# Value products of two heads side by side, bias rows read reversed, and a new order of the first microseconds

## The chip, the cores and the metric

One core of one Trainium2 chip runs the whole program: a two-layer block ("block 1") followed by another two-layer block ("block 2"), once. The metric is the device time of one execution in microseconds (us). Three executions of the kernel before gave 2213.95, 2214.05 and 2215.66 us; the median is 2214.05 us. The profile is of one further execution.

## What is computed

A sequence of 256 positions with 1024 features goes through two layers of block 1 and two of block 2. The change lies in block 1 alone. A layer of it, cut to what matters here:

```python
h = rms_norm(x, norm_mix_g[i])                  # (256, 1024)
proj = h @ w_in[i]                              # 10 thousand columns, cut into
q_r, k_r, v_r, g_r, q_n, kv_n, gate_n, m_a, m_b = split(proj)
o_r = retention(rotary(q_r), rotary(k_r), v_r)  # 4 heads
# 16 heads of "nsa" attention, 64 wide, two groups of keys and values:
#   logits of a query with the keys, plus a bias looked up by distance, softmax, times the values,
#   for three branches (compressed blocks, selected blocks, window), gated and added
x = x + mixer(o_r, nsa, m_a, m_b) @ w_out[i]
x = x + ffn(rms_norm(x, norm_ffn_g[i]))
```

The bias of a head depends only on the distance of query and key: `bias[q, k] = table[bucket(q - k), head]`. For 256 positions it is a row of 384 numbers for each head, of which query `q` reads a stretch of 256 that moves by one from query to query.

## The kernel before

**Weights and TensorE.** Activations are held transposed, as a part `hi` rounded to the short fp32 format (fp32r) and the rest `lo`. A weight piece of 512 KB comes in by DMA from SP's queue (`load`, L372), is split by ScalarE (`whi`, L169) and VectorE (`wlo`, L183), and is then multiplied in three products, hi with hi, hi with lo and lo with hi (`mm`, L216). Five raw pieces and six split ones are held. Each engine works through its own list in order, so an instruction that waits holds up all that stands behind it on that engine.

**The order.** `items` is a list of weight pieces and small steps. `execute` runs it, loads pieces and splits them up to `LOOK` ahead, and after each item `bg.pump` lets background generators (`bg`: one for each attention head and retention head) go on. A generator yields at points where it would have to wait; when it goes on is decided by a running estimate of each engine's clock (`eng`, fed by `use`), so the cost that `mm` notes for a product moves later instructions about.

**The start.** `load_x(0)`, a warm-up of `WARM` = 7 products on zeros, the identity matrix (`const_0`), and then the first norm: `Norm.__init__` has the gain row `norm_mix_g` copied to all 128 partitions by a DMA that reads the row 128 times (`bcast_row`, L589, 512 KB), ScalarE squares x (`half`), GpSimd takes the power (`power`, L239), VectorE multiplies x by scale and gain (`scale`, L194), TensorE transposes (`turn`, L250), and ScalarE and VectorE write `hi` and `lo` of it. `norm().both(0)` and `first_turn` do the first 128 positions; `lead` is the item from which weights are loaded and split, and it stands behind the first turn. Then come `load_x(1)`, the norm of the other 128 positions, and `const_1` with the tables for rotary and retention.

**The bias.** `make_bias` computes the 16 rows of 384 numbers by a product and writes them to DRAM as `rb` (L708). `spread(j)` then, for two heads at a time and eight times in all, reads two rows of `rb` into all 128 partitions (L713, `z<-rb`, 384 KB) and writes them out to DRAM as `bd` (L715, 384 KB), both from GpSimd's queue, so that every head has 128 equal rows of 384. `nsa_head` (L873) reads from `bd` with a row step of 383: the diagonal stretch. From the third pair on one `spread` is let go every `PACE` = 9 us, and head `h` begins only when "bias ready" has passed it.

**A head.** `nsa_head(qd, hh)` is head `hh` (0 to 3) of quad `qd` (0 to 3); two heads are under way at a time. Logits come by products with the keys `KH` and `KL`; VectorE adds the bias and takes the minimum in one operation (`add_max`, L203); ScalarE takes the exponential; the result `Z` is scaled, transposed by TensorE into `PT`, and multiplied with the values. That last step, the value products, is four products for a head: two branches, each with 256 and with 128 columns, with `vnat` as weights, 64 columns wide. Full fp32 products are run as two instructions each, so one head has eight instructions `b<-z,vnat`. Their output is the upper or the lower 64 partitions of the bank `O`, as the head's number is odd or even:

```python
if hh == 0: Q["O"] = bank([128, 2, 256])
e, c = hh % 2, hh // 2
o = slice(64 * e, 64 * e + 64)
for br in range(2):
    mm(O[o, c, :], vnat[:, 0, vs], PT[:, 256*br:256*br + 256], ...)
    mm(O[o, c, 128:], vnat[:, 1, vs], PT[:, 512 + 128*br:640 + 128*br], ...)
```

`Z` and `PT` come from a ring of six tiles (`zt`), `bias` from one of four.

Of the kernel before, what the change touches and what calls it, by code (L numbers as in the profile page):

```python
# [18 lines left out]
D = 1024  # L19
# [11 lines left out]
def _const_arrays():  # L31
# [13 lines left out]
    pack(0, [("ident", np.eye(128))])  # L45
# [6 lines left out]
    for h in range(4):  # L52
# [3 lines left out]
             ("decay", np.stack(dec, 1)), ("vmask", p[:, None] // 16 == np.arange(4)[None, :]), ("valid", p >= 31),  # L56
             ("fold", p[:, None] % 32 == np.arange(32)[None, :])])
# [34 lines left out]
WARM = 7  # L92
# [6 lines left out]
PACE = 9.0  # L99
# [3 lines left out]
def tile_kernel(ctx: ExitStack, tc: tile.TileContext, A: dict, out: bass.AP):  # L103
# [111 lines left out]
    def mm(o, lhsT, rhs, start, stop):  # L215
        nc.tensor.matmul(o, lhsT, rhs, start=start, stop=stop, skip_group_check=True)  # L216
        n = width(rhs)
        if rhs.dtype == F32R:
            ns = n / 2.4 * (1 if n >= 256 else 4)
        else:  # L220
            ns = n / 0.6 * width(lhsT) / 128
        use("P", ns, [o], [lhsT, rhs])
# [168 lines left out]
    def execute():  # L391
# [8 lines left out]
        for i, it in enumerate(items):  # L400
# [4 lines left out]
            while nxt < len(specs) and i >= lead:  # L405
# [7 lines left out]
                if turn is not None and sum(1 for q in specs if turn < q < j) >= PAST_TURN:  # L413
                    break
# [179 lines left out]
    class Norm:  # L594


        def __init__(self, row, dst, then=None):
            self.g = u([128, D])
            bcast_row(self.g, row, D)
# [13 lines left out]
        def scale(self, t):  # L613
# [3 lines left out]
            for c in range(2):  # L617
                cs = slice(512 * c, 512 * c + 512)
                self.xn[t, c] = x[:, t, cs] if self.dst is None else w2([128, 512])
                stt(out=self.xn[t, c], in0=x[:, t, cs], scalar=r, in1=self.g[:, cs], op0=OP.mult, op1=OP.mult)  # L620
# [53 lines left out]
    def load_x(t):  # L674
        for c in range(2):
            nc.sync.dma_start(x[:, t, 512 * c:512 * c + 512], xin[:, t, 512 * c:512 * c + 512])

    def begin():
        consts(cp, 0)


    def block1_constants():
        bp = S["bp"]
        consts(bp, 1)
# [5 lines left out]
    def make_bias():  # L690
# [12 lines left out]
        mm(b, tab, oneh[:, :384], True, True)  # L703
        bs = w2([16, 384])
        copy_v(bs, b)

        rb = dr.tile([16, 384], F32, name="rb")
        nc.sync.dma_start(rb, bs)  # L708
        S["bd"] = dr.tile([16, 128, 384], F32, name="bd")

        def spread(j):
            row = zt([128, 2, 384])
            nc.gpsimd.dma_start(row, bass.AP(tensor=rb.tensor, offset=rb.offset + 384 * j,  # L713
                                             ap=[[0, 128], [384, 2], [1, 384]]))
            nc.gpsimd.dma_start(S["bd"][j:j + 2].rearrange("h p k -> p h k"), row)  # L715

# [7 lines left out]
        spread(0)  # L724
# [5 lines left out]
        spread(2)  # L730
        arrives(rv, 12.0)
# [4 lines left out]
        for j in range(4, 16, 2):  # L736
            spread(j)
            S["bias ready"] = j
            step[0] = eng["P"] + PACE
            yield  # L740
        S["bias ready"] = 16

    def block1_layer(i):
# [122 lines left out]
        def nsa_head(qd, hh):  # L866
            g, h, Q = qd // 2, 4 * qd + hh, QD[qd]
            while len(flags) < 2 or S.get("bias ready", 0) <= h:
# [3 lines left out]
            bd = S["bd"]  # L872
            nc.gpsimd.dma_start(bias, bass.AP(tensor=bd.tensor, offset=bd.offset + 49152 * h + 127,  # L873
                                              ap=[[383, 128], [1, 256]]))
# [65 lines left out]
            if hh == 0:  # L940
                Q["O"] = bank([128, 2, 256])
            O = Q["O"]
            e, c = hh % 2, hh // 2
            o = slice(64 * e, 64 * e + 64)
            for br in range(2):
                vs = slice(128 * br + 64 * g, 128 * br + 64 * g + 64)
                mm(O[o, c, :], vnat[:, 0, vs], PT[:, 256 * br:256 * br + 256], c == 0 and br == 0, False)
                mm(O[o, c, 128:], vnat[:, 1, vs], PT[:, 512 + 128 * br:640 + 128 * br], False, False)
            Q["pv"] += 1
# [118 lines left out]
        proj_N(w, 7424, 256, "hT", 8, ev_values, runs=2, stride=384, tmajor=True, between=second_turn)  # L1068
        do(pos_turn)
# [733 lines left out]
    do(load_x, 0)  # L1803
    do(warm_up, WARM)
    do(begin)
    open_pool("block1")
    new_norm(A["norm_mix_g"][0], "hT")
    do(lambda: norm().both(0))
    first_turn("hT")
    lead = len(items)  # L1810
    do(load_x, 1)
# [37 lines left out]
```

## Time and profile before

| what | value |
|---|---|
| median of three executions | 2214.05 us |
| the profiled execution | 2216.03 us |
| its span, first to last instruction | 2214.3 us |
| TensorE busy | 2167.8 us, 98% |
| VectorE busy | 1486.1 us, 67% |
| ScalarE busy | 1236.4 us, 56% |
| moved by DMA | 383.31 MB |
| chain that ended last | TensorE 83%, VectorE 9%, ScalarE 3%, DMA 2% |

The profile shows one execution. PE is TensorE's products, PEld its weight loads, DVE VectorE, ACT ScalarE, POOL GpSimd, SP the engine that issues most DMAs (SPq its queue). A line number is a line of the kernel, often that of a helper (`mm` is L216, `act` L169, `tt` L183), so tiles tell more than lines. A row such as `b<-z,vnat` says that tile b was written from tiles z and vnat. Products are pipelined, and the ends that the profile gives for them are modelled; how long TensorE was taken up by a group is read from its start to the start of the next group. PEclk is the share of TensorE's full clock that was granted: 1.00 is 2.4 GHz, 0.50 is 1.2 GHz.

### The profile page before, as it was taken

How to read it: one execution, taken by the hardware profiler on the slowest of the kernel's cores; microseconds unless marked ns; L12 is line 12 of the kernel's file. 1: busy time of each engine (PE TensorE's matmuls, PEld its weight loads, DVE VectorE, ACT ScalarE, POOL GpSimd, SP SyncE). 2: the span in 40 equal slices, each digit the busy share in tenths (PEclk: the TensorE clock that was granted, in tenths of full speed). 3: DMA queues.
4: the chain of work that ended last, by engine and by line, in shares of the span. 5: the costliest groups of instructions: out<-in, count | busy, mean ns of one | idle time of the engine just before them, and what ended most of it. 6: DMA issues, size and time to landing. Idle time of an engine off the chain costs nothing.

```text
span 2214.3 us, 37531 instructions
## 1 busy us (share of the span) xinstructions
PE 2167.8 (98%) x14692; PEld 1973.1 (89%) x14692; DVE 1486.1 (67%) x2773; ACT 1236.4 (56%) x2044; POOL 115.0 (5%) x131
## 2 busy tenths in 40 slices
PE   8899999999999999999999999999999999989998
PEld 7688899899988888998998999988997999988997
DVE  5677765755576777666555887876557888776555
ACT  4466655544455566554444777655445777555443
POOL 2100100000000000000000010100000000100000
PEclk9999999999999999999999999999999999999999
DMA  9854455565676544555655545455655545455553
GB/s 299 281 150 132 141 153 156 176 199 187 194 223 178 150 139 141 146 180 179 185 187 169 175 134 172 139 174 179 190 188 171 165 144 173 147 163 180 190 186 109
DMA packets 299950, 383.31 MB, mean 173 GB/s; under 512 B 16635, under 2 KB 238987, under 8 KB 299772
## 3 DMA queue, kind: packets, MB, share of 16 engines
q1 hardware_dynamic: 296572, 370.12, 54.2%
q0 software_dynamic: 3200, 10.79, 1.5%
q8 instruction: 115, 1.88, 0.3%
q14 instruction: 63, 0.52, 0.1%
HBM read 376.60 MB, written 4.26 MB: 172 GB/s over the span
## 4 chain that ended last, share of the span: by engine, by line
PE 83%; DVE 9%; ACT 3%; DMA 2%; issue 2%; POOL 1%; SPq 0%; POOLq 0%; DVEq 0%; ACTq 0%
PE b L216 80%; DVE wlo L183 3%; PE b L250 3%; DMA raw<-w_in 2%; DVE u L183 2%; ACT z L169 1%; DVE w L183 1%; POOL s L239 1%; ACT u L169 1%; ACT whi L169 1%; DVE z L194 1%; DVE w L194 0%; DVE z L183 0%; ACT L169 0%; DMA w<-a_lambda 0%
## 5 line engine op out<-in xcount | busy, mean ns | idle before, releaser
L183 DVE TENSOR_TENSOR wlo<-raw,whi 128x1024 fp32r<-128x1024 f32 (+1 forms) x670 | 814.7, 1220 | 449.1 <-ACT whi L169 446.8
L169 ACT ACTIVATE whi<-raw 128x1024 fp32r<-128x1024 f32 (+1 forms) x670 | 704.2, 1056 | 656.8 <-PE b L216 464.7
L216 PE MATMUL b<-u,whi 128*128 128x256 f32 x5760 | 1052.8, 285 | 0.0
L216 PEld LDWEIGHTS b<-u,whi 128*128 128x128 f32 x5760 | 902.6, 192 | 10.0 <-issue 5.3
L216 PE MATMUL b<-u,wlo 128*128 128x256 f32 x2880 | 815.9, 283 | 0.0
L216 PE MATMUL b<-whi,u 128*128 128x512 f32 (+2 forms) x2752 | 811.6, 372 | 1.8 <-ACT whi L169 1.6
L216 PEld LDWEIGHTS b<-whi,u 128*128 128x128 f32 x2752 | 502.0, 189 | 90.9 <-issue 4.9
L216 PEld LDWEIGHTS b<-u,wlo 128*128 128x128 f32 x2880 | 552.7, 192 | 0.0
L216 PE MATMUL b<-wlo,u 128*128 128x512 f32 (+2 forms) x1376 | 509.5, 370 | 0.5 <-DVE wlo L183 0.5
L216 PEld LDWEIGHTS b<-wlo,u 128*128 128x128 f32 x1376 | 260.6, 189 | 39.6 <-DVE wlo L183 1.2
L169 ACT ACTIVATE u<-b 64x512 fp32r<-64x512 f32 (+3 forms) x234 | 133.0, 579 | 101.1 <-PE b L250 52.8
L239 POOL TENSOR_TENSOR s<-s,mhalf 128x1 f32<-128x1 f32 (+3 forms) x60 | 77.5, 1292 | 1508.2 <-DVE s L194 1047.1
L169 ACT ACTIVATE z<-z,s 128x256 f32<-128x256 f32 (+2 forms) x304 | 124.5, 425 | 51.6 <-DVE s L203 39.3
L183 DVE TENSOR_TENSOR u<-b,u 128x512 fp32r<-128x512 f32 (+2 forms) x150 | 98.3, 665 | 21.0 <-ACT u L169 16.8
L169 ACT ACTIVATE w<-b 128x512 f32<-128x512 f32 (+3 forms) x150 | 81.1, 547 | 43.2 <-PE b L216 42.0
L250 PE MATMUL b<-const,w 128*128 128x128 f32 (+1 forms) x416 | 65.3, 280 | 19.5 <-DVE w L194 9.3
L250 PEld LDWEIGHTS b<-const,w 128*128 128x128 f32 (+1 forms) x416 | 47.8, 141 | 31.5 <-issue 13.5
L216 PE MATMUL b<-u 128*128 128x256 f32 (+1 forms) x288 | 42.6, 293 | 14.8 <-ACT u L169 8.6
L169 ACT ACTIVATE u<-w 128x512 fp32r<-128x512 f32 x80 | 49.6, 619 | 11.5 <-DVE w L183 11.5
L216 PEld LDWEIGHTS b<-u 128*128 128x128 f32 x288 | 38.2, 196 | 18.5 <-ACT u L169 9.4
L183 DVE TENSOR_TENSOR w<-w 128x512 f32<-128x512 f32 (+3 forms) x94 | 51.9, 566 | 4.0 <-ACT w L169 3.7
L216 PE MATMUL b<-z,vnat 128*64 128x128 f32 (+1 forms) x256 | 46.8, 332 | 0.0
(145 smaller groups left out, 1233.2 us busy)
## 6 DMA issues: line engine op xcount, KB each, us to landing
raw<-w_in SPq DMA_DIRECT2D x268, 512.0 KB, 3.9
raw<-w_ffn_in SPq DMA_DIRECT2D x80, 512.0 KB, 3.6
raw<-w_up SPq DMA_DIRECT2D x64, 512.0 KB, 3.7
raw<-w_down SPq DMA_DIRECT2D x64, 512.0 KB, 3.5
raw<-w_ffn_out SPq DMA_DIRECT2D x44, 512.0 KB, 3.7
raw<-w_o_ret SPq DMA_DIRECT2D x32, 512.0 KB, 3.4
raw<-w_out SPq DMA_DIRECT2D x32, 512.0 KB, 3.8
raw<-w_o_nsa SPq DMA_DIRECT2D x16, 512.0 KB, 3.4
```

What stands on the lines that cost most here:

```text
L169: nc.scalar.activation(o, i, func, bias=bias, scale=scale, accum_out=accum_out)
L183: nc.vector.tensor_tensor(out=out, in0=in0, in1=in1, op=op)
L194: nc.vector.scalar_tensor_tensor(out=out, in0=in0, scalar=scalar, in1=in1, op0=op0, op1=op1)
L216: nc.tensor.matmul(o, lhsT, rhs, start=start, stop=stop, skip_group_check=True)
L239: nc.gpsimd.tensor_tensor(o, i, mhalf[:, :n], op=OP.pow)
L250: nc.tensor.transpose(o, i, C("ident")[:i.shape[0], :i.shape[0]])
```

## The change

Six edits, all in block 1 or ahead of it:

- **Paired value products.** An even head leaves its `PT` in `Q["PT"]` and ends; the odd head issues both heads' products, alternating: 256 columns of the even head, 256 of the odd, 128 of the even, 128 of the odd, for each branch. The planner books half the time for each (`share` 0.5).
- **Reversed bias rows.** `make_bias` writes the rows to DRAM back to front (`copy_v(bs, b[:, ::-1])`). A head then reads them directly from `rb` with a row step of 1, and takes the tile back to front (`bias[:, ::-1]`) as an operand of `add_max`. All eight `spread`s, `bd` and `PACE` go; heads wait for one flag.
- **The first gain row.** `norm_mix_g` comes in as one row of 4 KB, and TensorE spreads it to 128 partitions by a product with a row of ones, into two PSUM banks; `scale` reads it from there.
- **x in two queues.** The first half of x is issued from SP's queue and the second, with the gain row ahead of it, from ScalarE's, both at the start.
- **One piece ahead of the first turn.** `lead` moves ahead of `first_turn`; `FIRST` = 1 lets one weight piece be split before it. `WARM` is 3.
- **Constants.** Three small tables move from `const_1` to `const_0`; `const_1` is loaded behind the first projection.

The core of the diff:

```diff
-WARM = 7
+WARM = 3
+FIRST = 1
-PACE = 9.0
@@ execute
-                if turn is not None and sum(1 for q in specs if turn < q < j) >= PAST_TURN:
+                if turn is not None and sum(1 for q in specs if turn < q < j) >= (FIRST if turn == lead else PAST_TURN):
@@ Norm
-        def __init__(self, row, dst, then=None):
-            self.g = u([128, D])
-            bcast_row(self.g, row, D)
+        def __init__(self, row, dst, then=None, g=None):
+            if g is None:
+                rows = u([128, D])
+                bcast_row(rows, row, D)
+                g = [rows[:, :512], rows[:, 512:]]
+            self.g = g
@@ begin
+        for q, t in ((nc.sync, 0), (nc.scalar, 1)):
+            if t:
+                row = u([1, D])
+                q.dma_start(row, A["norm_mix_g"][0:1, :])
+            for c in range(2):
+                q.dma_start(x[:, t, 512 * c:512 * c + 512], xin[:, t, 512 * c:512 * c + 512])
+        ones = cp.tile([1, 128], F32, name="ones")
+        nc.vector.memset(ones, 1.0)
+        consts(cp, 0)
+        warm_up(WARM)
+        g = [bank([128, 512]) for _ in range(2)]
         for c in range(2):
-            nc.sync.dma_start(x[:, t, 512 * c:512 * c + 512], xin[:, t, 512 * c:512 * c + 512])
+            mm(g[c], ones, row[:, 512 * c:512 * c + 512], True, True)
+        S["norm"] = Norm(None, Act(8), g=g)
@@ make_bias
-        copy_v(bs, b)
+        copy_v(bs, b[:, ::-1])
-        def spread(j):
-            row = zt([128, 2, 384])
-            nc.gpsimd.dma_start(row, bass.AP(tensor=rb.tensor, offset=rb.offset + 384 * j,
-                                             ap=[[0, 128], [384, 2], [1, 384]]))
-            nc.gpsimd.dma_start(S["bd"][j:j + 2].rearrange("h p k -> p h k"), row)
...
-        for j in range(4, 16, 2):
-            spread(j)
-            S["bias ready"] = j
-            step[0] = eng["P"] + PACE
-            yield
-        S["bias ready"] = 16
+        S["bias ready"] = True
@@ nsa_head
-            nc.gpsimd.dma_start(bias, bass.AP(tensor=bd.tensor, offset=bd.offset + 49152 * h + 127,
-                                              ap=[[383, 128], [1, 256]]))
+            rb = S["rb"]
+            nc.gpsimd.dma_start(bias, bass.AP(tensor=rb.tensor, offset=rb.offset + 384 * h + 1,
+                                              ap=[[1, 128], [1, 256]]))
+            bias = bias[:, ::-1]
...
-            if hh == 0:
+            Q["pv"] += 1
+            if hh % 2 == 0:
+                Q["PT"] = PT
+                return
+            if hh == 1:
                 Q["O"] = bank([128, 2, 256])
+            O, c = Q["O"], hh // 2
+            pair = [(slice(0, 64), Q.pop("PT")), (slice(64, 128), PT)]
             for br in range(2):
                 vs = slice(128 * br + 64 * g, 128 * br + 64 * g + 64)
-                mm(O[o, c, :], vnat[:, 0, vs], PT[:, 256 * br:256 * br + 256], c == 0 and br == 0, False)
-                mm(O[o, c, 128:], vnat[:, 1, vs], PT[:, 512 + 128 * br:640 + 128 * br], False, False)
+                for o, P in pair:
+                    mm(O[o, c, :], vnat[:, 0, vs], P[:, 256 * br:256 * br + 256], c == 0 and br == 0, False, 0.5)
+                for o, P in pair:
+                    mm(O[o, c, 128:], vnat[:, 1, vs], P[:, 512 + 128 * br:640 + 128 * br], False, False, 0.5)
```

The planner places the value products anew. On TensorE, the first of them in the first layer stood by themselves in the kernel before (`z` is the transposed `PT` of one head, `kh`, `kl` the keys, `whi`, `wlo` a weight piece):

```order
L216 MATMUL b_1386<-kh0_166,u_553 128x256
L216 MATMUL b_1386<-kl0_168,u_553 128x256
L216 MATMUL b_1399<-z_1345,vnat_171 64x256
L216 MATMUL b_1399<-z_1345,vnat_171 64x128
L216 MATMUL b_1399<-z_1345,vnat_171 64x256
L216 MATMUL b_1399<-z_1345,vnat_171 64x128
L216 MATMUL b_1410<-whi_1327,u_92 128x512
```

Now the same place, the first value products on TensorE in the first layer, reads:

```order
L216 MATMUL b_1408<-whi_1371,u_95 128x512
L216 MATMUL b_1464<-z_1360,vnat_171 64x256
L216 MATMUL b_1464<-z_1415,vnat_171 64x256
L216 MATMUL b_1464<-z_1360,vnat_171 64x128
L216 MATMUL b_1464<-z_1415,vnat_171 64x128
L216 MATMUL b_1464<-z_1360,vnat_171 64x256
L216 MATMUL b_1464<-z_1415,vnat_171 64x256
L216 MATMUL b_1464<-z_1360,vnat_171 64x128
L216 MATMUL b_1464<-z_1415,vnat_171 64x128
L216 MATMUL b_1401<-whi_1395,u_97 128x512
```

The products of two heads (`z_1360` and `z_1415`) alternate with nothing between them; all 16 pairs of the two layers stand so.

On GpSimd, from the norm of the second 128 positions on, the kernel before has (`rc` holds the compressed branch's bias, `s` small tiles of the norm):

```order
L239 TENSOR_TENSOR s_157<-s_156,mhalf_72 128x1
L723 DMA rc_269<-w_267 128x5x16
L713 DMA z_271<-rb_258 128x768
L728 DMA z_274<-rc_269 128x16x16 x2
L713 DMA z_277<-rb_258 128x768
L715 DMA bd_260<-z_271 128x2x384
L713 DMA z_430<-rb_258 128x768
L715 DMA bd_260<-z_277 128x2x384
```

And now, on the same engine from the same norm on:

```order
L239 TENSOR_TENSOR s_159<-s_158,mhalf_72 128x1
L730 DMA rc_268<-w_266 128x5x16
L734 DMA z_270<-rc_268 128x16x16 x2
L873 DMA bias_1086<-rb_258 128x256
L873 DMA bias_1088<-rb_258 128x256
L873 DMA bias_1438<-rb_258 128x256
```

All transfers `z<-rb` and `bd<-z` (eight of each) are gone, and the heads' reads come directly from `rb`.

On VectorE, the first instructions with data were before:

```order
L194 SCALAR_TENSOR_TENSOR s_104<-s_98 128x1
L194 SCALAR_TENSOR_TENSOR w_108<-x_74,s_105,u_96 128x512
L194 SCALAR_TENSOR_TENSOR w_110<-x_74,s_105,u_96 128x512
L183 TENSOR_TENSOR u_93<-b_112,u_92 128x4x128
L183 TENSOR_TENSOR u_95<-b_119,u_94 128x4x128
L183 TENSOR_TENSOR wlo_130<-raw_126,whi_129 128x1024
L183 TENSOR_TENSOR wlo_137<-raw_133,whi_136 128x1024
```

The first instructions of VectorE with data are now:

```order
L194 SCALAR_TENSOR_TENSOR s_108<-s_99 128x1
L183 TENSOR_TENSOR wlo_120<-raw_116,whi_119 128x1024
L194 SCALAR_TENSOR_TENSOR w_112<-x_74,s_109,b_91 128x512
L194 SCALAR_TENSOR_TENSOR w_114<-x_74,s_109,b_92 128x512
L194 SCALAR_TENSOR_TENSOR s_158<-s_100 128x1
L194 SCALAR_TENSOR_TENSOR w_162<-x_74,s_159,b_91 128x512
L183 TENSOR_TENSOR u_96<-b_126,u_95 128x4x128
L183 TENSOR_TENSOR u_98<-b_133,u_97 128x4x128
L194 SCALAR_TENSOR_TENSOR w_164<-x_74,s_159,b_92 128x512
L183 TENSOR_TENSOR wlo_141<-raw_123,whi_140 128x1024
```

The split of the first weight piece (`wlo_120`) has moved ahead of the norm's products with x, and three instructions of the other positions' norm (`s_158`, `w_162`, `w_164`) ahead of the second piece's split (`wlo_141`).

## Rows read from the trace of the kernel before

**Rows 1.** Page: busy us, share, instructions by engine; ScalarE's weight splits.

```profile
PE 2167.8 (98%) x14692; PEld 1973.1 (89%) x14692; DVE 1486.1 (67%) x2773; ACT 1236.4 (56%) x2044; POOL 115.0 (5%) x131
...
L169 ACT ACTIVATE whi<-raw 128x1024 fp32r<-128x1024 f32 (+1 forms) x670 | 704.2, 1056 | 656.8 <-PE b L216 464.7
```

**Rows 2.** Stretches: length, busy us (count) by engine, PEclk, DMA share, GB/s.

```profile
0.00:5.00 5.00, 3.53 (x8) 2.86 (x9) 0.73 (x4) 2.68 (x5) 0.19 (x4) 1.00 0.45 150
5.00:10.00 5.00, 2.52 (x12) 1.97 (x11) 1.41 (x2) 0.00 (x0) 0.55 (x1) 0.86 0.94 324
...
50.00:70.00 20.00, 19.81 (x149) 16.69 (x147) 11.18 (x15) 8.55 (x12) 7.45 (x12) 1.00 1.04 390
70.00:80.00 10.00, 2.42 (x9) 2.13 (x10) 8.82 (x11) 6.16 (x8) 0.00 (x0) 0.67 1.07 367
80.00:90.00 10.00, 10.00 (x49) 7.89 (x48) 3.44 (x8) 4.46 (x9) 0.00 (x0) 0.81 0.69 210
110.00:290.00 180.00, 180.00 (x1160) 158.64 (x1159) 139.69 (x416) 119.53 (x263) 15.68 (x25) 1.00 0.48 142
```

**Rows 3.** TensorE in time: start us, us, instruction, [idle before <-releaser].

```profile
138.44 1.51 PE L216 MATMUL b<-z,vnat 128*64 128x256 f32 x8
139.88 0.50 PE L216 MATMUL b<-whi,u 128*128 128x512 f32 x1
...
290.65 2.22 PE L216 MATMUL b<-z,vnat 128*64 128x256 f32 x16
292.80 0.39 PE L216 MATMUL b<-u,whi 128*128 128x256 f32 x1
...
370.92 1.51 PE L216 MATMUL b<-z,vnat 128*64 128x256 f32 x8
...
957.50 1.51 PE L216 MATMUL b<-z,vnat 128*64 128x256 f32 x8
```

**Rows 4.** Tile vnat: instructions, duration min/median/max, first and last start.

```profile
L216 PE MATMUL b<-z,vnat x256: 272/326/431, 138.4 to 958.7; 128*64 128x256 f32 x64, 128*64 128x128 f32 x64
```

**Rows 5.** TensorE in time: an attention of block 2 with alternating halves.

```profile
1275.55 0.88 PE L216 MATMUL b<-z,V 128*64 128x256 f32 x8
1276.35 0.39 PE L216 MATMUL b<-u 128*128 128x256 f32 x1
```

**Rows 6.** TensorE in time, 69 to 79 us.

```profile
69.42 0.39 PE L216 MATMUL b<-whi,u 128*128 128x512 f32 x1
77.29 0.79 PE L216 MATMUL b<-u 128*128 128x256 f32 x2 [7.49 <-ACT u L169]
78.37 1.01 PE L216 MATMUL b<-u 128*128 128x256 f32 x3 [0.28 <-DVE u L183]
```

**Rows 7.** Chain that ended last, 30 to 90 us: start, us, what.

```profile
57.74 12.82 DMA raw<-w_in
```

**Rows 8.** DMA of 0 to 100 us: queue; issues, KB, median to landing.

```profile
q0 software_dynamic: 1856, 7.12, 19.5%
...
z<-rb POOLq DMA_DIRECT2D x8, 384.0 KB, 7.9
bd<-z POOLq DMA_DIRECT2D x8, 384.0 KB, 6.8
```

**Rows 9.** TensorE in time, its early waits and the first product of layer 1.

```profile
12.66 0.80 PE L216 MATMUL b<-whi,u 128*128 128x512 f32 x1 [1.63 <-ACT whi L169]
...
40.04 0.67 PE L216 MATMUL b<-z 128*128 128x512 f32 x1 [0.75 <-DMA z<-rc]
...
622.19 0.48 PE L216 MATMUL b<-whi,u 128*128 128x512 f32 x1
```

**Rows 10.** VectorE in time, 8 to 18 us.

```profile
8.25 1.41 DVE L194 SCALAR_TENSOR_TENSOR w<-x,s,u 128x512 f32<-128x512 f32 x2 [3.29 <-DMA u<-norm_mix_g]
...
12.64 4.63 DVE L183 TENSOR_TENSOR wlo<-raw,whi 128x1024 fp32r<-128x1024 f32 x4 [0.25 <-ACT whi L169]
```

**Rows 11.** Tile bias: bias additions, duration min/median/max, first and last start.

```profile
L203 DVE CUSTOM_DVE_ANT_0 z<-b,bias x128: 248/285/294, 121.6 to 948.9; 128x128 f32<-128x128 f32 x128
```

## What the change will do to the time

> **What bounds the kernel now.** I began with the shares on the page: TensorE is busy for 98% of the span, VectorE for 67% [rows 1]. That is an average, so I went on to the table of stretches. From 110 to 290 us, where the first layer's heads run, TensorE is busy for all of 180 us at the full clock, while VectorE is idle for 40 of them and DMA works at half its share [rows 2]. There, time is what TensorE is given to do. The stretch from 70 to 80 us is the exception: TensorE is busy for 2.4 of 10 us, the DMA engines are full (share 1.07, as in the 20 us before), and the granted clock falls to 0.67 and stays low into the next stretch [rows 2]. TensorE's own rows show one wait of 7.49 us [rows 6], and the chain of waits leads from it, through the splits and rotary steps that stand in VectorE's list, back to a weight piece that was issued at 57.74 us and took 12.82 us to land [rows 7]. At the very start a third picture: VectorE waits 3.29 us for the copied gain row, and TensorE's first real product starts at 12.66 us [rows 9, 10]. The sum below has a term for each of the three.
>
> **Paired value products.** Each head has eight instructions, 256 in all, so 32 heads [rows 4]. A head by itself occupies TensorE from 138.44 to 139.88 us, 1.44 us; all lone heads look like this. Two places have two heads back to back in their old order, 2.15 us from 290.65 to 292.80 [rows 3]. So 28 lone heads and two doubles cost 28 x 1.44 + 2 x 2.15 = 44.6 us. What a pair in the new form costs is shown by an attention of block 2 that already writes the upper and the lower half of a bank with the same shapes: its eight instructions, one branch of two heads, take from 1275.55 to 1276.35, 0.80 us [rows 5]. A lone head needs 1.44 us for two branches, so if its first branch costs 0.80 like that pair's, its second costs 0.64; the pair takes no longer than the lone head, and the halves run at the same time. I take 1.45 us for a pair with both branches. Sixteen pairs: 23.2 us. The term is **-21.4 us**. It lies on the path whole, because TensorE has no idle time in these stretches. Ends: 1.35 us a pair by the two doubles, where overlap goes on through the middle of the group (-23), and 1.80 for the rival below (-15.8). What covers the rest: VectorE's work is not less, and its 140 us then stand in about 170 instead of 180 us, still with idle time.
>
> TensorE's list in block 2 has the alternating products in another order (256 and 128 columns of one half, then of the other), and the row of 0.80 us says that the halves overlap even so [rows 5]. The Trainium skill, in "TensorE: Matmul & The Clock Gate", section "Part 3: Packing small matmuls — row/col tiling", says that products start and end strictly in program order and only weight loads are pulled ahead. By that rule two full-fp32 products, each two passes, would overlap only where the second pass of one half meets the first of the other, and the pairs would give 15.8 instead of 21.4 us. The row speaks against it here; it is kept as a rival.
>
> **Spreads and the bias.** Eight reads `z<-rb` and eight writes `bd<-z` of 384 KB go [rows 8]: 16 x 0.393 = 6.3 MB of the 7.12 MB that the software queue moved. At the 390 GB/s of 50 to 70 us [rows 2] that is 16 us of full DMA, all of it ahead of the wait at 69.7 us or beside it. The wait is 7.49 us, so twice as much transfer goes as is needed to end it. With it go 0.28 us of idle at 78.37 [rows 6] and the low clock after it: 0.81 over 80 to 90 us is 3.8 us at half clock [rows 2], and the 2.7 us from 77.29 to 80 are at half clock too; less the idle, 6.2 us of which half are lost, 3.1. Together 7.5 + 0.3 + 3.1 = **-10.9 us**. A further 0.75 us, the wait for `z<-rc` at 40.04 [rows 9], goes with the full queues: **-0.75**. What is late next there is TensorE itself. `const_1` (786 KB, 2 us of DMA) stands later in SP's queue than before, ahead of the pieces for 30 us on; it is not needed before the rotary steps. Bounds: nothing gained but half of the wait (-5.5), and, on the other side, all that the first layer takes longer than the second. From its first product to its last value product the first layer takes 370.92 - 12.66 = 358.3 us, the second 957.50 - 622.19 = 335.3 [rows 3, 9]; the 23 us are the most that this and the next part could give.
>
> Per head the read from `rb` moves as much as that from `bd`. It is issued 3 us of planner's time ahead, and a later landing would hold VectorE, which has slack, before TensorE. Reading an operand back to front is not in the trace. The bias additions take 285 ns [rows 11], 192 in all with a second form; I take no change, since each still reads one element after the other, and price the opposite below.
>
> **The start.** The copied gain row (512 KB) goes and the second half of x takes its place ahead of the first weight piece, so about as many bytes stand before it: two halves of x, 0.084 of constants and the piece, 1.66 MB. By 5 us 0.75 MB had moved, and then 324 GB/s [rows 2], which puts the piece at 5 + 0.91/0.324 = 7.8 us. VectorE's list now has that piece's split ahead of the norm's products: 7.8 + 1.06 (ScalarE) [rows 1] + 1.16 (VectorE, 4.63/4) [rows 10] = 10.0 us, where before the norm's products began at 8.25. From there to the first product it was 12.66 - 8.25 = 4.4 us; the split on ScalarE (1.06) and the second half of the norm (about 0.7, half of 1.41 us) no longer stand in between, which leaves 2.6 and puts the first product at about 12.6 us: no earlier. What remains is that both parts of the first piece are ready and that the second turn's work is done in between, against three norm instructions (1.5 us) that now stand ahead of the second piece's split. I take **-1 us**, with -2.5 (piece at 7.0 us) and +2 (piece where it was, above 9 us, everything behind it) as ends. The two spreading products and the shorter warm-up lie in TensorE's wait and cost nothing; the clock was low after the long warm-up too (0.86 over 5 to 10 us [rows 2]), so I expect the same low start. ScalarE issues three DMAs ahead of its table load, some 1.3 us, while x is on its way.
>
> **Sum.** -21.4 - 10.9 - 0.75 - 1.0 = -34. The profiled execution took 2216.03 us (span 2214.3 and 1.7 around it), 2.0 more than the median of 2214.05; against the profile the sum gives 2182, against the median **2180 us**.
>
> **Rivals.**
> - *Halves only overlap in part.* Products issue in strict order. Count a pass of 256 columns as a step: a lone head takes 6 steps in 1.44 us, two heads one after the other 12, and a pair in which only the second pass of one half meets the first of the other 7.5, which is 1.80 us; 16 x 1.80 = 28.8, and the saving is 44.6 - 28.8 = 15.8: **2186 us**. For it: no trace of before has this very order of full-fp32 pairs. Against it: the 0.80 us of [rows 5].
> - *The DMA wait stays in part, or the start comes late.* Weight pieces, x and `const_1` alone fill the queues, or the first piece lands at 9 us: 5 to 8 us less, **2185 to 2188**. Against it: 6.3 MB less, and the next layer has no such wait.
> - *More goes.* If the first layer becomes like the second save for its bias products, 5 to 10 us more: **2170 to 2175**.
> - *Held tiles.* The even head's `PT` stays in the ring of six until the odd one is done; two heads under way hold four, so five of six are in use. If that delays each pair by 0.5 to 1 us, **2188 to 2196**.
> - *Slower: VectorE becomes the bound.* If an operand read back to front is slow, 96 additions a layer grow. VectorE's idle time of 40 us from 110 to 290 [rows 2], less the 11 by which the stretch shrinks, is used up at +0.31 us each; from +0.49 us (2.7 times as long) the gain is gone, and at three times (+0.57) it is 2 x (55 - 30) = 50 us against the 34: **2230 us**.
>
> **How the numbers follow.** Forecast, 2175 to 2185: 0.62. More goes: 0.12. DMA or start in part: 0.12. Partial overlap: 0.06. Held tiles: 0.03. Slower by VectorE: 0.05. The range 2170 to 2188 leaves out the last two and the edges of the others. About 0.2%, 4.4 us, is what a measurement of this kernel can tell from no change; all cases but the last lie beyond it on the fast side, so faster 0.94, same 0.01 (a half-slow VectorE), slower 0.05.
>
> **What would show it.** In the profile of the changed kernel: 16 groups of sixteen value products at about 1.45 us each; if they take 1.8, it is the partial overlap. No idle of TensorE above 1 us between 20 and 300 us, and a granted clock of 1.00 from 70 to 90 us; a wait there with DMA share near 1 would be the second rival. Less software-queue traffic by 6.3 MB. First product between 11 and 14 us. Bias additions at 285 ns; if they are at 600 or more and VectorE is full from 110 to 290 us, the last rival has come. The prediction would be wrong if TensorE showed waits on `PT` or bias tiles in the heads' stretches.

## The result, and the profile after

| | kernel before | changed kernel |
|---|---|---|
| median of four executions each | 2214.86 us | 2179.26 us |
| lowest to highest | 2213.95 to 2216.77 us | 2178.75 to 2181.48 us |
| ratio of the times, 95% interval | | 0.984, 0.9823 to 0.9857 |
| span of the profiled execution | 2214.3 us | 2177.6 us |
| chain that ended last: TensorE, VectorE, DMA | 83%, 9%, 2% | 86%, 8%, 0% |

The change takes 35.6 us off; 2180 had been forecast. The page of the changed kernel: busy us, share and instructions by engine, then DMA queues with packets, MB and share, then the chain by engine.

```profile
PE 2142.6 (98%) x14688; PEld 1957.2 (90%) x14688; DVE 1487.1 (68%) x2774; ACT 1235.2 (57%) x2044; POOL 100.5 (5%) x115
...
q0 software_dynamic: 1664, 4.50, 1.2%
...
PE 86%; DVE 8%; ACT 3%; issue 1%; POOL 1%; DMA 0%; POOLq 0%; SPq 0%; DVEq 0%; ACTq 0%
```

TensorE is busy for 25.2 us less than in [rows 1]; the rest of the 36.7 us of span is its idle time. The software queue moves 4.50 MB over the whole span, 10.79 before: the 6.3 MB of the spreads are gone.

Stretches of the changed kernel: length, busy us (count) of PE, PEld, DVE, ACT and POOL, PEclk, DMA share, GB/s.

```profile
30.00:50.00 20.00, 20.00 (x165) 18.83 (x164) 14.30 (x31) 11.14 (x18) 4.49 (x6) 1.00 1.08 311
50.00:70.00 20.00, 20.00 (x151) 17.19 (x150) 16.56 (x22) 9.70 (x12) 0.00 (x0) 1.00 0.92 284
70.00:80.00 10.00, 10.00 (x55) 7.48 (x57) 5.47 (x11) 6.03 (x10) 0.00 (x0) 1.00 0.71 223
80.00:90.00 10.00, 10.00 (x57) 7.46 (x50) 5.56 (x9) 3.94 (x6) 0.79 (x2) 1.00 0.57 163
110.00:290.00 180.00, 180.00 (x1226) 162.15 (x1225) 142.41 (x447) 124.73 (x288) 13.25 (x25) 1.00 0.53 149
```

Against [rows 2]: TensorE fills 70 to 80 us, where it had 2.42 of 10; the clock is 1.00 in all of these stretches; the DMA share from 50 us on is 0.92 and falling, where it had been 1.04 and then 1.07.

TensorE of the changed kernel in time, around the first pair of value products: start us, us, instruction.

```profile
132.23 0.39 PE L216 MATMUL b<-whi,u 128*128 128x512 f32 x1
132.55 1.52 PE L216 MATMUL b<-z,vnat 128*64 128x256 f32 x16
134.00 0.50 PE L216 MATMUL b<-whi,u 128*128 128x512 f32 x1
134.34 0.40 PE L216 MATMUL b<-wlo,u 128*128 128x512 f32 x1
134.57 0.62 PE L216 MATMUL b<-whi,u 128*128 128x512 f32 x2
```

Two heads take from 132.55 to 134.00, 1.45 us; one head took 1.44 [rows 3]. All 16 groups look like this, 23.2 us in all.

Tile bias of the changed kernel: the additions (duration in ns min/median/max) and the landing of its transfers.

```profile
L203 DVE CUSTOM_DVE_ANT_0 z<-b,bias x128: 249/286/293, 108.7 to 908.8; 128x128 f32<-128x128 f32 x128
...
DMA to landing us min/median/max: 3.1/3.6/8.3
```

286 ns read back to front, 285 front to back [rows 11].

The start of the changed kernel, on ScalarE, VectorE and TensorE, one answer each: start us, us, instruction, idle before and its releaser.

```profile
8.40 1.06 ACT L169 ACTIVATE whi<-raw 128x1024 fp32r<-128x1024 f32 x1 [2.35 <-DMA raw<-w_in]
```

```profile
9.48 1.23 DVE L183 TENSOR_TENSOR wlo<-raw,whi 128x1024 fp32r<-128x1024 f32 x1 [3.25 <-ACT whi L169]
10.63 1.40 DVE L194 SCALAR_TENSOR_TENSOR w<-x,s,b 128x512 f32<-128x512 f32 x2
```

```profile
11.42 1.97 PE L250 MATMUL b<-const,w 128*128 128x128 f32 x8 [3.18 <-DVE w L194]
13.22 0.79 PE L216 MATMUL b<-whi,u 128*128 128x512 f32 x1
13.81 0.63 PE L216 MATMUL b<-wlo,u 128*128 128x512 f32 x1
```

The piece was there at 8.40 us instead of 7.8, and the first product came at 13.22 instead of 12.6. The 0.59 us between two products of 512 columns, against 0.34 and 0.23 in the stretch above, point to the low clock. The profile's clock column reads 1.00 there, but in e7 below, which has the same instructions up to there and the same 0.59 us, it reads 0.50 from 10 to 15 us.

**A ledger by landmarks.** TensorE's order differs between the kernels, but GpSimd takes the same powers for the norms in both. GpSimd of the kernel before, at three of them (first retention norm, norm ahead of the feed-forward part of layer 1, the last norm):

```profile
95.20 0.57 POOL L239 TENSOR_TENSOR s<-s,mhalf 128x1 f32<-128x1 f32 x1
...
1010.38 0.56 POOL L239 TENSOR_TENSOR s<-s,mhalf 128x1 f32<-128x1 f32 x1 [116.61 <-DVE s L194]
...
2187.71 1.46 POOL L239 TENSOR_TENSOR s<-s,mhalf 128x1 f32<-128x1 f32 x1 [6.12 <-DVE s L194]
```

The same in the changed kernel:

```profile
82.25 0.57 POOL L239 TENSOR_TENSOR s<-s,mhalf 128x1 f32<-128x1 f32 x1
...
973.50 0.56 POOL L239 TENSOR_TENSOR s<-s,mhalf 128x1 f32<-128x1 f32 x1 [116.43 <-DVE s L194]
...
2151.13 1.47 POOL L239 TENSOR_TENSOR s<-s,mhalf 128x1 f32<-128x1 f32 x1 [6.11 <-DVE s L194]
```

The same way for every kernel below, in us ahead of the kernel before (a minus is behind; the second column is the feed-forward norm of layer 0, 423.79 us before):

| kernel | 95 us | layer 0 | layer 1 | end | time, us |
|---|---|---|---|---|---|
| changed kernel | 13.0 | 25.0 | 36.9 | 36.6 | 2179.26 |
| e1, pairs alone | 3.6 | 15.8 | 27.7 | 24.2 | 2193.05 |
| e2, reversed bias alone | 12.2 | 12.4 | 12.4 | 9.8 | 2202.78 |
| e3, start alone | 4.5 | 4.6 | 4.7 | 3.4 | 2211.63 |
| e10, spreads back as traffic | 6.8 | 18.3 | 30.2 | 29.5 | 2190.49 |
| e8, spreads further apart | 5.0 | -11.4 | -11.4 | -11.4 | 2228.28 |
| e5, pairs not alternating | 12.0 | 18.4 | 24.6 | 24.2 | 2192.09 |
| e6, alternating by branch | 12.8 | 24.5 | 35.9 | 35.2 | 2181.01 |
| e7, planner's share 1.0 | 13.5 | 25.4 | 37.3 | 34.7 | 2181.73 |
| e4, no piece ahead of the turn | 11.6 | 23.7 | 35.6 | 34.4 | 2181.80 |
| e9, longer warm-up | 14.0 | 26.0 | 38.0 | 35.1 | 2180.21 |
| changed kernel, second profile | 12.5 | 24.5 | 36.4 | 35.9 | 2180.60 |

So 13.0 us come before 95 us, 12.0 in layer 0, 11.9 in layer 1, and block 2 gives back 0.3. Each row is one execution, set against one execution of the kernel before; how far two executions of the same instructions lie apart is seen in the first experiments.

### The profile page after: what moved, and what is told of

Read it like the earlier page. It is cut to its first block, busy times and chain, and to the rows that moved or that the text cites. A ratio compares the mean times of both kernels' runs of the same rounds, so it can differ in the third digit from the quotient of the medians.

```text
span 2177.6 us, 37496 instructions
## 1 busy us (share of the span) xinstructions
PE 2142.6 (98%) x14688; PEld 1957.2 (90%) x14688; DVE 1487.1 (68%) x2774; ACT 1235.2 (57%) x2044; POOL 100.5 (5%) x115
## 4 chain that ended last, share of the span: by engine, by line
PE 86%; DVE 8%; ACT 3%; issue 1%; POOL 1%; DMA 0%; POOLq 0%; SPq 0%; DVEq 0%; ACTq 0%
PE b L216 83%; PE b L250 3%; DVE wlo L183 3%; DVE u L183 2%; ACT z L169 1%; ACT u L169 1%; POOL s L239 1%; DVE w L183 1%; ACT whi L169 1%; DVE z L194 1%; DVE w L194 0%; DVE z L183 0%; ACT L169 0%; DVE z L1408 0%; DVE s L208 0%
## 5 line engine op out<-in xcount | busy, mean ns | idle before, releaser
L239 POOL TENSOR_TENSOR s<-s,mhalf 128x1 f32<-128x1 f32 (+3 forms) x60 | 73.1, 1219 | 1505.8 <-DVE s L194 1045.5
L183 DVE TENSOR_TENSOR u<-b,u 128x512 fp32r<-128x512 f32 (+2 forms) x150 | 98.2, 665 | 13.6 <-ACT u L169 10.8
L169 ACT ACTIVATE w<-x 128x512 f32<-128x512 f32 x44 | 27.4, 624 | 33.3 <-DVE x L183 30.6
```

The lines of the kernel that those rows point to most:

```text
L169: nc.scalar.activation(o, i, func, bias=bias, scale=scale, accum_out=accum_out)
L183: nc.vector.tensor_tensor(out=out, in0=in0, in1=in1, op=op)
L239: nc.gpsimd.tensor_tensor(o, i, mhalf[:, :n], op=OP.pow)
```

## The experiments

**Each part alone: e1, e2, e3.** e1 is the kernel before with the paired products of the diff and `share`; e2 is it with the reversed rows, without `spread` and `bd`; e3 is it with the edits of the start (gain row, x in two queues, `FIRST`, `WARM`, constants). Their diffs are the matching pieces of the one shown ahead.

> The kernel before with the paired value products alone. Theory (halves of the array run at the same time, TensorE is the limit): 16 groups of sixteen value products at 1.45 us, 21.5 us less there, 21 to 24 us in all, about 2191 to 2193 us, and the 7.5 us wait near 70 us stays. Rival (the pairs only pay off because the DMA wait went, or the held tiles cost something without the other edits): less than 15 us.

> The kernel before with the reversed bias rows alone: no spreads, heads read from rb. Theory (the spreads' 6.3 MB fill the DMA queues): the wait of 7.5 us near 70 us and the half clock behind it go, 10.9 + 0.75 = 11 to 12.5 us less, about 2202 to 2204 us; bias additions stay at 285 ns. Rival (the wait comes from the weights and const_1 alone): under 5 us.

> The kernel before with the edits of the start alone (gain row spread by TensorE, x in two queues, one piece ahead of the first turn, warm-up of 3, const_1 later). Theory: the start itself gives about 1 us (0 to 2.5), 2212 to 2215 us, and the wait near 70 us stays at 6 to 8 us. Rival (the bytes that are moved or spared at the start, half a megabyte, shorten the wait near 70 us): 3 us or more.

Measured: e1 2193.05 us, ratio 0.9902 (0.9885 to 0.9918); e2 2202.78, 0.9947 (0.9932 to 0.9962); e3 2211.63, 0.9983 (0.9973 to 0.9992). TensorE of e1 in time, with the wait near 70 us:

```profile
74.54 0.80 PE L216 MATMUL b<-u 128*128 128x256 f32 x2 [5.28 <-ACT u L169]
```

Stretches of e2:

```profile
50.00:70.00 20.00, 20.00 (x153) 17.23 (x151) 16.89 (x24) 10.83 (x13) 0.00 (x0) 1.00 0.96 307
70.00:80.00 10.00, 10.00 (x54) 7.85 (x53) 6.06 (x10) 5.27 (x10) 0.00 (x0) 1.00 0.68 213
```

TensorE of e3 in time (its line numbers are one higher):

```profile
40.67 1.10 PE L217 MATMUL b<-z 128*128 128x512 f32 x2 [2.98 <-issue]
...
72.17 0.51 PE L217 MATMUL b<-u 128*128 128x256 f32 x2 [1.74 <-ACT u L170]
```

e2 by itself ends the wait and the low clock after it. It is 12.2 us ahead at 95 us, and its median is 12.7 us below the 2215.50 us of the kernel before in the same series. e1 gains 12.2 and 11.9 us in the two layers; its median is 22.4 us lower.

The first column needs care. Up to 95 us, e1 has the same instructions in the same order as the kernel before, on every engine and in every DMA queue: its value products come later. Still it is 3.6 us ahead there, with a wait of 5.28 us where [rows 6] has 7.49. So these 3.6 us are a difference between two executions and not an effect of the pairs. With the spreads in place, the length of the wait near 70 us varies. Without them, five profiles whose lists are the same up to 95 us (the changed kernel's two, e5, e6, e7) stand at 12.0 to 13.5.

What the weight pieces took to land shows where the wait comes from. DMA issues of pieces from 45 to 70 us, in the kernel before, e1, e2 and the changed kernel: size of one, median us from issue to landing.

```profile
raw<-w_in SPq DMA_DIRECT2D x8, 512.0 KB, 13.8
```

```profile
raw<-w_in SPq DMA_DIRECT2D x8, 512.0 KB, 10.9
```

```profile
raw<-w_in SPq DMA_DIRECT2D x11, 512.0 KB, 5.2
```

```profile
raw<-w_in SPq DMA_DIRECT2D x9, 512.0 KB, 4.9
```

With the spreads a piece takes two to nearly three times as long. e3 still has them, and its pieces take 11.1 us. It has two waits, 1.74 us near 70 us and 2.98 at 40.67. The piece that its chain waits for was issued at 51.81 us and took 13.63 us, against 57.74 and 12.82 in [rows 7]: it came earlier, not faster. By its median e3 is 3.9 us lower (1.8 to 6.0 by the interval of its ratio). In the changed kernel the start adds less: 12.0 to 13.5 us at 95 us, against 12.2 for e2, is a gain between -0.2 and 1.3. Whether the start edits also shorten the spreads' wait, one profile of each can't tell from the difference between executions.

**The traffic alone: e10, e8.** e10 is the changed kernel with the sixteen spread transfers put back, which nobody reads; e8 is the kernel before with the spreads further apart.

```diff
+        S["bd"] = dr.tile([16, 128, 384], F32, name="bd")
+        def spread(j):
+            row = zt([128, 2, 384])
...
+        spread(0)
...
+        spread(2)
...
+        for j in range(4, 16, 2):
+            spread(j)
+            step[0] = eng["P"] + 9.0
+            yield
```

And e8:

```diff
-PACE = 9.0
+PACE = 27.0
```

> The changed kernel with the sixteen transfers of the spreads put back, whose result nobody reads; the heads still read rb and wait for one flag. Theory (bytes in the queues made the wait): a TensorE wait of several us near 70 us comes back, with DMA share near 1.05 from 30 to 70 us, 7 to 12 us more than the changed kernel, about 2186 to 2191 us. Rival (the wait came from the gate and the pace of 9 us, or from heads that waited for bd): 0 to 2 us more.

> The kernel before with PACE = 27 instead of 9: the same sixteen spread transfers, but the last six pairs come three times as far apart in the planner's clock. Theory (the wait near 70 us is the bias traffic in front of the weight pieces): the DMA share over 50 to 70 us falls from 1.04 to 0.95 or less, the wait of 7.5 us shrinks below 3 us, and by the GpSimd landmark at 95 us the kernel is 5 to 12 us ahead of the kernel before; time 2203 to 2211. Rival (what counts is the long chain of a spread's landing, rb to tile to bd, not how much stands in the queues): the wait near 70 us stays at 6 us or more, time 2213 to 2218. Third: the heads are held back by the late rows and the planner fills with other work, which moves waits to 100 to 200 us.

Measured: e10 2190.49 us (ratio 0.9885, 0.9871 to 0.99), e8 2228.28 (1.0056, 1.0039 to 1.0072). Stretches of e10:

```profile
50.00:70.00 20.00, 17.41 (x129) 14.30 (x127) 16.30 (x23) 11.70 (x16) 6.17 (x10) 1.00 1.04 396
70.00:80.00 10.00, 9.30 (x41) 7.48 (x42) 3.97 (x7) 4.98 (x8) 0.00 (x0) 0.66 1.10 349
```

TensorE of e10 in time:

```profile
70.42 0.79 PE L216 MATMUL b<-u 128*128 128x256 f32 x2 [3.01 <-ACT u L169]
```

Weight pieces of e10 from 45 to 70 us, as above:

```profile
raw<-w_in SPq DMA_DIRECT2D x9, 512.0 KB, 9.7
```

No engine but GpSimd, which issues them, waits for these transfers, and up to 95 us the lists of all other engines are those of the changed kernel. Still the wait is back, the clock falls, a piece takes 9.7 us to land instead of 4.9, and by 95 us 13.0 - 6.8 = 6.2 us are lost (5.2 to 6.7 against the five profiles above). The profiled execution is the fastest of e10's four, 2186.45 us; by the medians the loss is 11.2 us. It is the transfers in the queues that hold up the weight pieces.

In e8 only five of the eight pairs are out before 56 us, its weight pieces land in 8.0 us, and its wait near 70 us is down. TensorE of e8 in time, at 70 us and later:

```profile
73.23 0.50 PE L216 MATMUL b<-u 128*128 128x256 f32 x2 [2.16 <-ACT u L169]
...
274.00 0.33 PE L250 MATMUL b<-const,z 128*128 128x128 f32 x1 [2.71 <-DVE z L188]
...
378.51 1.36 PE L250 MATMUL b<-const,z 128*128 128x128 f32 x4 [3.52 <-ACT z L169]
```

That gives 5.0 us by 95 us, but only 1.4 more than e1, whose lists are those of the kernel before; and the DMA share over 50 to 70 us is 1.05, where the theory had 0.95 or less. So e8 fits the theory in part and does not decide by itself. Its time missed the forecast. The rows of the later heads come late (the last pair is read at 202.88 us on GpSimd), the last heads' value products run until after 390 us instead of 371, and TensorE waits for the heads' own steps at 274 and 378 us. From 380 to 390 us no weight products are left to lie between them. In all, 16.4 us are lost in layer 0. That is the third outcome, later than forecast.

**The order within a pair: e5, e6, e7.** e5 issues all eight products of the even head and then all eight of the odd one; e6 issues, for each branch, 256 and 128 columns of the even head, then of the odd one; e7 has `share` 1.0. The diffs against the changed kernel, in this order:

```diff
-            for br in range(2):
-                vs = ...
-                for o, P in pair:
+            for o, P in pair:
+                for br in range(2):
+                    vs = ...
                     mm(O[o, c, :], ...)
-                for o, P in pair:
                     mm(O[o, c, 128:], ...)
```

```diff
                 for o, P in pair:
                     mm(O[o, c, :], ...)
-                for o, P in pair:
                     mm(O[o, c, 128:], ...)
```

```diff
-        use("P", ns * share, [o], [lhsT, rhs])
+        use("P", ns, [o], [lhsT, rhs])
```

> The changed kernel with the sixteen value products of a pair in another order: all eight of the even head, then all eight of the odd one, still back to back. Theory (the two halves run at the same time when products of both are near each other in TensorE's list; how far apart they may stand is the question): as in the two doubles of the kernel before, 2.15 us a group instead of 1.45, that is 16 x 0.7 = 11 us more than the changed kernel, about 2190 us. Rival (any order back to back overlaps in full): 1.45 us a group and no change, 2179 us. Rival (strict program order): 2.7 us a group, 20 us more.

> The changed kernel with the order of block 2 within each pair: for a branch 256 and 128 columns of the even head, then 256 and 128 of the odd one. Theory (products of the two halves overlap over a distance of four instructions, as block 2's 0.80 us a branch shows): 1.45 to 1.6 us a group, 0 to 2 us more than the changed kernel, 2179 to 2182 us. Rival (strict program order): 1.8 us or more a group, 6 us or more.

> The changed kernel with the planner booking the whole time for each product of a pair (share 1.0 instead of 0.5), so that the order of the instructions differs but not their number. Theory (what the pairs give is run time on TensorE, not the planner's order): 16 groups of sixteen at 1.45 us, no wait above 1 us from 20 to 300 us, time 2177 to 2185. Rival (the planner's order gave a part): a new wait between 100 and 400 us, the end of layer 0 at least 2 us later than in the changed kernel, time 2186 or more.

Measured, one execution each: 2192.09, 2181.01 and 2181.73 us. TensorE of e5 in time, the first group:

```profile
133.50 2.22 PE L216 MATMUL b<-z,vnat 128*64 128x256 f32 x16
135.66 0.50 PE L216 MATMUL b<-whi,u 128*128 128x512 f32 x1
```

Value products of that group that are at work from 133.45 to 134.20 us, and from 134.38 to 134.42 (duration in ns min/median/max, first and last start):

```profile
L216 PE MATMUL b<-z,vnat x4: 272/326/430, 133.5 to 134.1; 128*64 128x256 f32 x2, 128*64 128x128 f32 x2
...
L216 PE MATMUL b<-z,vnat x2: 379/405/431, 134.2 to 134.2; 128*64 128x256 f32 x2
```

And e6, the same group:

```profile
132.73 1.57 PE L216 MATMUL b<-z,vnat 128*64 128x256 f32 x16
134.24 0.50 PE L216 MATMUL b<-whi,u 128*128 128x512 f32 x1
```

e6 takes 1.50 us a group, close to the 1.45 of full alternation; e5 takes 2.15, which is what two adjacent heads took before. In e5 four products start alone, the first with 430 ns, the next of 256 columns with 379. At 134.2 us two of 256 columns begin together, with 379 and 431. The second is the odd head's first, ninth in TensorE's list: it starts beside the even head's fifth, ahead of three that stand before it. So the even head's second half and the odd head's first half run together, and the overlap reaches over about four products; e6's distance of two is within it. That each engine works through its list in order, as the part on the kernel before has it, does not hold for TensorE's two halves here. The Trainium skill, "TensorE: Matmul & The Clock Gate", section "Part 3: Packing small matmuls — row/col tiling", says that products start and end strictly in program order; by that, e6 could overlap only where its halves meet, and e5 in one place. The rows of both disagree with it for the start. e7, with another order of the rest, has the same 1.45 us groups and no wait; its ledger is 0.4 to 0.5 us ahead of the changed kernel's up to layer 1. What the pairs give is TensorE's own time and not the planner's order.

**The start: e4, e9.** e4 is the changed kernel with `FIRST` = 0; e9 has four more warm-up products behind the spreading ones, in TensorE's wait. e9 was run once, and then four times beside the unaltered changed kernel; the table has it by its second profile.

```diff
-FIRST = 1
+FIRST = 0
```

```diff
+        warm_up(4)
         S["norm"] = Norm(None, Act(8), g=g)
```

> The changed kernel without a weight piece split ahead of the first turn. Theory (the norm's products stand behind that split in VectorE's list and wait for it from about 8.0, when scale and gain are ready, to 10.63 us): they start near 8 us, the first transposes near 9 us instead of 11.42, the first product of weights at 11 to 12.5 us instead of 13.22; 0 to 2 us less. Rival (the edit pays): the first product has to wait for the split afterwards, at 13 us or later, and nothing or less than nothing is gained.

> The changed kernel with four more products on zeros behind the two that spread the gain row, in TensorE's wait from 8.2 to 11.4 us. Theory (TensorE's clock goes to full the sooner the less it idles before): the products of 512 columns follow each other at 0.23 us from about 13 us on instead of from 16.6, 1 to 2.5 us less. Rival (the clock rises no sooner): 0.42 us a product until 16 us or later, and no change or up to 1 us more where the zeros' products hold up the transposes.

> The kernel of e9_warm_more, timed: four more warm-up products behind the spreading ones, in TensorE's wait for the norm. In its single look the spacing of products was that of the full clock from 13.1 us (16.6 in the changed kernel) and the landmark at 95 us stood 1.3 us earlier, while the end stood where the changed kernel's stands. Theory: the 1.3 us are real and the two later half-clock stretches of block 2 vary between executions, so over five rounds 2176 to 2179, 1 to 2 below the changed kernel of the same job. Rival: block 2 gives them back each time, and the two agree within 0.5 us.

> The changed kernel unaltered, on the same chip as e9_timed, as its measure: 2178.5 to 2181.5 as in its first runs. The half-clock stretches of block 2 should stand at other places or have other lengths than in its first profile if they vary between executions, and at the same places if they hang on the order of the work.

Measured: e4 2181.80 us (one execution); e9 2179.83 (one execution) and then 2180.21 (median of four, ratio 0.9836, 0.9822 to 0.9851); the changed kernel beside it 2180.60 (0.9838, 0.9823 to 0.9853). TensorE of e4 in time:

```profile
11.83 0.80 PE L216 MATMUL b<-whi,u 128*128 128x512 f32 x1 [1.63 <-ACT whi L169]
...
20.93 0.50 PE L216 MATMUL b<-wlo,u 128*128 128x512 f32 x1
21.27 0.62 PE L216 MATMUL b<-whi,u 128*128 128x512 f32 x2
```

TensorE of e9, timed:

```profile
8.17 3.78 PE L216 MATMUL b<-w 128*128 128x256 f32 x8
11.74 1.92 PE L250 MATMUL b<-const,w 128*128 128x128 f32 x8
13.49 0.55 PE L216 MATMUL b<-whi,u 128*128 128x512 f32 x1
13.88 0.40 PE L216 MATMUL b<-wlo,u 128*128 128x512 f32 x1
```

e4's first product comes 1.4 us before the changed kernel's, but its products stand at the spacing of half clock until 20.9 us (16.6 in the changed kernel), and at 95 us it is 0.8 to 1.3 us behind the two profiles of the changed kernel, 0.3 to 1.8 behind the five that share their lists up to there. The early split is worth about that, as far as one execution shows. e9 fills TensorE's wait; its products follow at 0.39 us from 13.5 us on and at the full clock's spacing from 13.9, and it is 1.5 us ahead of the second profile at 95 us and 1.6 at the end of layer 1. At the end it is 0.8 behind. Stretch 1170 to 1190 us of e9, and then of the changed kernel beside it (columns as above):

```profile
1170.00:1190.00 20.00, 17.91 (x86) 14.97 (x86) 13.90 (x23) 12.05 (x17) 1.95 (x2) 0.91 0.48 136
```

```profile
1170.00:1190.00 20.00, 17.79 (x90) 14.52 (x90) 13.62 (x22) 12.87 (x21) 1.96 (x2) 1.00 0.41 123
```

Both wait 2.09 us for VectorE here, at 1176.7 and 1178.3. In e9 the granted clock falls behind it, in the other kernel it doesn't. Block 2 took most of e9's lead back in both of its profiles, and the two times agree: the rival in its expectation. No experiment gave a time measurably below the changed kernel's.

## Why the prediction was right, point by point

- **Paired value products: right.** 16 groups of 1.45 us were forecast and measured. The choice between 1.45 and 1.80, which went by the row of another attention [rows 5] against the rule of strict order, was the right one; e5 and e6 show why. The layers give 12.0 and 11.9 us, though, where the groups alone explain 10.8 each (read start to start, they add up to 22.4 us a layer before and 11.6 now). The other 1.1 to 1.2 a layer had no term. In the rows above, a value product starts 0.32 us after the `whi` product before it, and the one behind the group takes 0.34, where weight products among themselves follow at 0.23: each border of a group costs up to 0.1 us, and there are 16 groups where there were 30. e5 agrees: a layer before has 14 lone groups and a double, 22.4 us, and e5 has 8 x 2.15 = 17.2; the 5.2 between them are less than the 6.4 and 6.2 that it gains. That the borders are all of it is argued from these rows, not tried apart.
- **Spreads: right in mechanism, and in size within what varies.** 10.9 + 0.75 = 11.65 us were forecast; e2 has 12.2 at 95 us against the profile of before, 8.6 against e1's, and 12.7 by its median (8.4 to 15.1 by the interval of its ratio). The term was read from one wait of 7.49 us; e1's 5.28 for the same instructions would have made it 2.2 smaller by the wait alone. e10 shows that the transfers do it, without any wait of TensorE for them. "Twice as much transfer goes as is needed" held: without the spreads nothing is late in their place, and TensorE no longer waits there.
- **The start: the size is about right, the working only in part.** -1 was taken; 13.0 - 12.2 = 0.8 came out, 0.3 by the second profile, and these are within the 1.5 us by which profiles with the same lists differ. The piece landed 0.6 us later than worked out, and all behind it moved by the same 0.6. That the first product comes no earlier held. That the second turn's work done in between pays all the same is borne out by e4, in one execution. The expectation for e3 that the wait near 70 us would stay at 6 to 8 us was wrong, and its time came out below the forecast; why is open, as said there.
- **Slack of the heads: right.** From 20 to 420 us TensorE's waits come to 0.4 us in all, none on `PT` or on bias tiles; VectorE is busy for 142.4 of 180 us from 110 to 290 us, and the reversed operand costs 1 ns.
- **What hid between the terms.** The parts were summed as if each had its own time. Alone they are 22.4, 12.7 and 3.9 us faster by their medians, 39.0 in all, against 35.6 together. The intervals of the ratios reach 2 to 4 us to either side, so the 3.4 us between show neither that parts share a wait nor that they don't. By the end of layer 1 the three are 27.7 + 12.4 + 4.7 = 44.8 us ahead alone and 36.9 together, but 3.6 of that is e1's other execution, and most of the rest lies in e3's 4.5 by 95 us. That the total came within 1 us of 2180 is in part luck: from profile to profile 36.45 us went, not 34, with 2.5 more than forecast from the pairs.
- **Block 2** is the same code at another time, and no term was kept for it. It gave back 0.3 and 0.5 us in the two profiles of the changed kernel, 3.5 in e1, 2.6 in e2, 1.3 in e3, and 1.8 and 2.9 in the two of e9, which have the same instructions throughout.

## What to carry over

When two heads write the two halves of a bank, issue their products within a few instructions of each other: alternating halves doubled the rate here, and adjacent heads in sequence gave only half of the gain. Transfers that nobody is waiting for can still be the cause of a wait, when they stand in full queues ahead of those that somebody needs; look at what stands ahead of the late transfer and how long it took to land, not at waits on the early ones. Read each part by a landmark that all the kernels share, but before a lead there is put down to an edit, see whether the instructions up to it differ at all: two executions of the same instructions lay 3.6 us apart at 95 us here.

## What the chip showed that was not expected

- Products that write other columns of the array started ahead of products before them in TensorE's list: in e5 the ninth of a group began beside the fifth, at 134.2 us.
- The wait near 70 us took 7.49 us in one execution and 5.28 in another with the same instructions up to there, and weight pieces landed in 13.8 and 10.9 us. Without the spreads, five profiles with the same lists stay within 1.5 us at 95 us.
- The granted clock behind one and the same wait of 2.09 us fell in e9 (0.91 over 20 us) and stayed at 1.00 in the changed kernel. Such falls in block 2 were seen in e1, e2, e5, e7 and e9 between 1177 and 1206 us, and not in the others; the ledger falls by up to 3.5 us from there to the end, other falls included. The Trainium skill, "TensorE: Matmul & The Clock Gate", section "Part 1: The HAM clock gate (the "warmup" mystery)", says that what watches TensorE's activity runs freely, not from the kernel's start, so the same kernel meets it at other points each time. Two profiles of the changed kernel with low stretches of block 2 at other places (from 1426 us in the first, from 1403 and 1430 in the second) agree with that; no run here tests it, and what decided each fall stays open.
- Warm-up products in the norm's wait brought the full clock 1 to 5 us earlier (at 13.1 and 13.6 us, and at 15.0 to 17.6 in five profiles without them), and the 1.5 us gained did not reach the end.
